# A batched mixture-of-experts kernel: the planner's part closed after two loads, semaphores by hand, experts in pairs, TensorE in one loop

## The chip, the cores and the metric

The kernel runs on one core of a Trainium2 chip. A core has five engines with instruction streams of their own: TensorE (PE; its weight loads are listed as PEld), VectorE (DVE), ScalarE (ACT), GpSimd (POOL) and SyncE (SP). Data comes from and goes to the chip's main memory (HBM) through 16 DMA engines. [...] The metric is the device time of one execution in microseconds (us), lower is better.

## The reference

There are 8 experts. Each multiplies its 256 rows of 512 numbers by its own first matrix, clips at zero, and multiplies by its own second matrix. Everything arrives and leaves as float32.

```python
n_experts, capacity, hidden, expert_hidden = 8, 256, 512, 2048
# x: (8, 256, 512)   w1: (8, 512, 2048)   w2: (8, 2048, 512), float32
h = np.matmul(x, w1)
h = np.maximum(h, 0)
return np.matmul(h, w2).astype(np.float32)
```

Per expert, `w1` and `w2` have 4.19 MB each. All weights together are 67.1 MB, `x` is 4.19 MB and the output is 4.19 MB.

## The kernel before

The kernel is written in Tile, a layer that allocates buffers from pools, finds the dependences between instructions and adds the semaphore waits. `manual_schedule` (line 48) keeps the instructions of each engine in the order of the source, so the order of the calls in lines 144 to 192 is the order of the queues.

A weight matrix is one load: 128 partitions, each with 32 KB of float32 that is contiguous in HBM, written to SBUF as bfloat16 (16 KB per partition, 2048 KB in all). `load_w1` (line 67) and `load_w2` (line 71) issue these loads on POOL. `wpool` gives each of the two tags three buffers (`WB = 3`), so a load waits until the expert three before it has been used. Only the last two `w2` are cut in two (line 73): expert 6 after 8 of its 16 blocks, expert 7 after 9.

`x` is taken in four groups (line 34). Experts 0 and 1 come as float32 on SP into `x_f` and are cast to bfloat16 by ACT (lines 145, 155, 156). Experts 2 and 3, and then 4 to 7, come on POOL with the cast made by the DMA (line 65). `transpose_x` (line 77) turns the blocks of `x` with TensorE, 64 transposes in all, and DVE or ACT copy them from PSUM to `xt`.

`first_layer(e)` (line 102) makes the hidden values in four steps of 16 matmuls; after each step ACT or DVE applies the clipping while it moves the result from PSUM to `ht`. `second_layer(e)` (line 124) runs 32 matmuls over the 16 blocks of `w2`, then DVE and ACT copy the two halves of the output to `o_sb`. For most experts the second layer follows the first. At the end all first layers are done before: 5, 6, 7 first layers, then second layers 5, 6, 7 (lines 183 to 191), and the loads stand in the same order: `w1` of 5, 6 and 7, then `w2` of 5, 6 and 7.

The output leaves in three stores: experts 0 to 4 and 5 to 6 on POOL, where they stand behind all loads of weights (lines 187 and 190), and expert 7 on SP (line 192). When the function returns, Tile closes: SP waits for every semaphore in use, then all engines meet at two barriers with the semaphores cleared in between (line 218).

TensorE's stream is unrolled: 832 matmuls (64 transposes, 512 of the first layer, 256 of the second), each with a weight load of its own, 1664 instructions.

Of the kernel before, what the change touches and what calls it, by code (L numbers as in the profile page):

```python
# [7 lines left out]


@with_exitstack  # L10
def kernel(
    ctx: ExitStack,
    tc: tile.TileContext,
    x: bass.AP,
    w1: bass.AP,
    w2: bass.AP,
    out: bass.AP,
):
    nc = tc.nc
    P = 128  # L20
    bf = mybir.dt.bfloat16
    f32 = mybir.dt.float32
    relu = mybir.ActivationFunctionType.Relu

    E, C, H = x.shape
    F = w1.shape[2]
    MT = C // P
    KT1 = H // P
    KT2 = F // P
    FB = 4  # L30
    WB = 3


    GROUPS = ((0, 1), (1, 1), (2, 2), (4, 4))


    w1_r = w1.rearrange("e (p kt) n -> e p kt n", p=P)
    w2_r = w2.rearrange("e (p kt) n -> e p kt n", p=P)
    out_r = out.rearrange("e (p mt) n -> p e mt n", p=P)

    const = ctx.enter_context(tc.tile_pool(name="const", bufs=1))
    wpool = ctx.enter_context(tc.tile_pool(name="weights", bufs=WB))
    hpool = ctx.enter_context(tc.tile_pool(name="hidden", bufs=3))
    ps_h = ctx.enter_context(tc.tile_pool(name="ps_h", bufs=2, space=bass.MemoryType.PSUM))
    ps_o = ctx.enter_context(tc.tile_pool(name="ps_o", bufs=4, space=bass.MemoryType.PSUM))


    ctx.enter_context(tc.manual_schedule())

    w1_sb, w2_sb, ht = {}, {}, {}  # L50
    group_of = {e: g for g, (e0, n) in enumerate(GROUPS) for e in range(e0, e0 + n)}
    x_f = const.tile([P, 2, MT, H], f32, name="x_f")
    x_b = [const.tile([P, n * MT, H], bf, name=f"x_b{g}") for g, (_, n) in enumerate(GROUPS)]
    xt = [const.tile([P, KT1, MT, n * P], bf, name=f"xt{g}") for g, (_, n) in enumerate(GROUPS)]
    o_sb = const.tile([P, E, MT, H], f32, name="out_sb")
    identity = const.tile([P, P], bf, name="identity")

    def x_rows(g):
        e0, n = GROUPS[g]
        return x[e0:e0 + n].rearrange("e c k -> (e c) k").rearrange(  # L60
            "(p j) k -> p j k", p=P
        )

    def load_x(g):
        nc.gpsimd.dma_start(x_b[g][:], x_rows(g))  # L65

    def load_w1(e):
        w1_sb[e] = wpool.tile([P, KT1, F], bf, tag="w1", name="w1_sb")
        nc.gpsimd.dma_start(w1_sb[e][:], w1_r[e])  # L69

    def load_w2(e):
        w2_sb[e] = wpool.tile([P, KT2, H], bf, tag="w2", name="w2_sb")
        cuts = {E - 2: (0, 8, 16), E - 1: (0, 9, 16)}.get(e, (0, KT2))
        for lo, hi in zip(cuts, cuts[1:]):
            nc.gpsimd.dma_start(w2_sb[e][:, lo:hi, :], w2_r[e, :, lo:hi, :])  # L75

    def transpose_x(g, blocks=None):


        n = GROUPS[g][1]  # L80
        J = n * MT
        KB = 8 // J
        for b in blocks if blocks is not None else range(KT1 // KB):
            pt = ps_o.tile([P, KB, J, P], bf, tag="ps_o", name="pt_tr")
            for i in range(KB):
                for j in range(J):
                    nc.tensor.transpose(  # L87
                        pt[:, i, j, :], x_b[g][:, j, b * KB + i::KT1], identity[:]
                    )
            for i in range(KB) if n > 1 else (slice(0, KB),):  # L90
                if n > 1:
                    src = pt[:, i].rearrange("p (l m) q -> p l m q", m=MT)
                    dst = xt[g][:, b * KB + i].rearrange("p m (q l) -> p l m q", l=n)
                    flip = b * KB + i
                else:
                    src, dst, flip = pt[:, i], xt[g][:], g
                if flip % 2:
                    nc.scalar.copy(dst, src)  # L98
                else:
                    nc.vector.tensor_copy(dst, src)  # L100

    def first_layer(e, between=()):
        g = group_of[e]
        i0 = (e - GROUPS[g][0]) * P
        ht[e] = hpool.tile([P, KT2, C], bf, tag="ht", name="ht_sb")
        for q in range(KT2 // FB):
            ph = ps_h.tile([P, FB, C], f32, tag="ps_h", name="pt_h")
            for i in range(FB):
                for kt in range(KT1):
                    nc.tensor.matmul(  # L110
                        ph[:, i, :],
                        w1_sb[e][:, kt, FB * q + i::KT2],
                        xt[g][:, kt, :, i0:i0 + P],
                        start=(kt == 0),
                        stop=(kt == KT1 - 1),
                    )
            if q % 2:
                nc.vector.tensor_relu(ht[e][:, FB * q:FB * (q + 1), :], ph[:])  # L118
            else:
                nc.scalar.activation(ht[e][:, FB * q:FB * (q + 1), :], ph[:], relu)  # L120
            if between:
                between.pop(0)()

    def second_layer(e):
        po = [
            ps_o.tile([P, H], f32, tag="ps_o", name=f"pt_o{mt}") for mt in range(MT)
        ]
        for kt in range(KT2):
            for mt in range(MT):
                nc.tensor.matmul(  # L130
                    po[mt][:],
                    ht[e][:, kt, mt * P:(mt + 1) * P],
                    w2_sb[e][:, kt, :],
                    start=(kt == 0),
                    stop=(kt == KT2 - 1),
                )
        nc.vector.tensor_copy(o_sb[:, e, 0, :], po[0][:])  # L137
        nc.scalar.copy(o_sb[:, e, 1, :], po[1][:])  # L138

    def store(e0, e1):  # L140
        nc.gpsimd.dma_start(out_r[:, e0:e1], o_sb[:, e0:e1])  # L141


    for e in (0, 1):
        nc.sync.dma_start(x_f[:, e], x_rows(e))
    load_w1(0)
    make_identity(nc, identity)
    load_w2(0)
    load_x(2)
    load_w1(1)  # L150
    load_w2(1)
    load_x(3)
    load_w1(2)
    load_w2(2)
    nc.scalar.copy(x_b[0][:], x_f[:, 0])  # L155
    nc.scalar.copy(x_b[1][:], x_f[:, 1])  # L156
    transpose_x(0)

    first_layer(0)
    load_w1(3)  # L160
    transpose_x(1)
    second_layer(0)
    load_w2(3)
    first_layer(1)
    load_w1(4)
    transpose_x(2)
    second_layer(1)
    load_w2(4)
    first_layer(2, [lambda kt=kt: transpose_x(3, [kt]) for kt in range(KT1)])
    load_w1(5)  # L170
    second_layer(2)
    first_layer(3)
    load_w1(6)
    second_layer(3)
    first_layer(4)
    load_w1(7)
    load_w2(5)
    load_w2(6)
    second_layer(4)
    load_w2(7)  # L180


    for e in (5, 6, 7):
        first_layer(e)


    store(0, 5)
    second_layer(5)
    second_layer(6)
    store(5, 7)  # L190
    second_layer(7)
    nc.sync.dma_start(out_r[:, 7], o_sb[:, 7])


# [28 lines left out]
```

## Time and profile before

| | us |
|---|---|
| median of 3 runs (lowest, highest) | 182.62 (182.59, 183.62) |
| span of the profiled execution, first to last instruction | 180.5 |
| TensorE busy with matmuls | 127.1 |
| ScalarE busy | 31.6 |
| VectorE busy | 31.8 |
| GpSimd busy | 13.1 |

The times are whole executions. The span runs from the first to the last instruction of the program, and the difference, 2.1 us against the median, lies around the span. In the views below a releaser is what ended a wait, "xN" is a number of instructions, and a DMA share of 1.00 means that all 16 DMA engines have work all the time. GB/s counts bytes as they are written, so a load that turns float32 into bfloat16 reads twice what the column shows.

### The profile page before, as it was taken

Reading aid. Unit: us, or ns where it says so; the run is one execution under the profiler, and the core shown is the slowest. Engines: PE = TensorE matmul, PEld = TensorE weight load, DVE = VectorE, ACT = ScalarE, POOL = GpSimd, SP = SyncE. Lnnn points to the kernel's source line nnn. Section 1 sums busy time; section 2 is a strip of 40 time slices with the busy share of each in tenths; the row PEclk is TensorE's granted clock in tenths of the full one; section 3 lists DMA queues with packets and bytes.
Section 4 is the critical chain, followed back from the end, with each engine's and each line's share of the span. In section 5 each row is a group of like instructions: output and inputs, shape, how many; then the busy total and the mean of one; then the engine's idle time right before and its main releaser. Section 6 shows DMA issues by size and latency. Waiting matters only on the chain.

```text
span 180.5 us, 1824 instructions
## 1 busy us (share of the span) xinstructions
PE 127.1 (70%) x832; PEld 89.1 (49%) x832; DVE 31.8 (18%) x29; ACT 31.6 (18%) x32; POOL 13.1 (7%) x28
## 2 busy tenths in 40 slices
PE   0206989059992199978778594979498968997910
PEld 0105964049840189538633591449387953442400
DVE  0100220102401028510501022012204230101010
ACT  3300230102221027512201130012122220101010
POOL 7300010100101000100100004030000000001000
PEclk9999999957999669999999997899969999999995
DMA  6998999999999899999999998999999999999994
GB/s 222 243 229 178 232 232 200 207 232 207 200 232 229 182 229 232 214 192 232 229 200 211 232 225 185 229 232 214 192 232 229 192 218 207 225 211 206 369 421 184
DMA packets 4246, 40.47 MB, mean 224 GB/s; under 512 B 400, under 2 KB 400, under 8 KB 1936
## 3 DMA queue, kind: packets, MB, share of 16 engines
q0 software_dynamic: 3808, 38.80, 96.9%
q1 hardware_dynamic: 432, 1.57, 2.3%
q8 instruction: 6, 0.10, 0.2%
HBM read 71.30 MB, written 4.19 MB: 418 GB/s over the span
## 4 chain that ended last, share of the span: by engine, by line
DMA 46%; PE 38%; another core or an unknown queue 9%; POOL 2%; issue 1%; ACT 0%; POOLq 0%
DMA w_sb<-in_w_dram 46%; PE pt_o L130 18%; PE pt_h L110 18%; PE pt_tr L87 2%; POOL w_sb L75 1%; POOL w_sb L69 0%; ACT out_sb L138 0%; POOL x_b L65 0%; POOL identity masks.py:199 0%; POOL identity masks.py:197 0%; POOLq masks.py:199 0%; POOLq L207 0%
## 5 line engine op out<-in xcount | busy, mean ns | idle before, releaser
L110 PE MATMUL pt_h<-xt,w_sb 128*128 128x256 bf16 x512 | 65.3, 293 | 30.7 <-DMA w_sb<-in_w_dram 30.7
L110 PEld LDWEIGHTS <-w_sb 128*128 128x128 bf16 x512 | 59.7, 147 | 36.9 <-DMA w_sb<-in_w_dram 33.9
L130 PE MATMUL pt_o<-w_sb,ht_sb 128*128 128x512 bf16 x256 | 58.2, 387 | 9.4 <-DMA w_sb<-in_w_dram 9.4
L130 PEld LDWEIGHTS <-ht_sb 128*128 128x128 bf16 x256 | 25.2, 99 | 40.6 <-issue 11.3
L118 DVE TENSOR_SCALAR ht_sb<-pt_h 128x1024 bf16<-128x1024 f32 x16 | 19.6, 1228 | 65.8 <-PE pt_h L110 65.8
L120 ACT ACTIVATE ht_sb<-pt_h 128x1024 bf16<-128x1024 f32 x16 | 16.5, 1032 | 69.2 <-PE pt_h L110 69.2
L138 ACT COPY out_sb<-pt_o 128x512 f32<-128x512 f32 x8 | 4.7, 585 | 62.5 <-PE pt_o L130 62.5
L137 DVE COPY out_sb<-pt_o 128x512 f32<-128x512 f32 x8 | 5.5, 692 | 57.2 <-PE pt_o L130 57.2
L69 POOL DMA_DIRECT2D w_sb<-in_w_dram x8 | 4.5, 556 | 85.3 <-PE pt_h L110 84.5
L100 DVE COPY xt<-pt_tr 128x1024 bf16<-128x1024 bf16 (+1 forms) x5 | 7.1, 1446 | 18.0 <-PE pt_tr L87 18.0
L87 PE MATMUL pt_tr<-identity,x_b 128*128 128x128 bf16 x64 | 5.4, 238 | 5.1 <-ACT x_b L155 5.1
L98 ACT COPY xt<-pt_tr 128x1024 bf16<-128x1024 bf16 (+1 forms) x5 | 7.4, 1502 | 6.6 <-PE pt_tr L87 4.0
L87 PEld LDWEIGHTS <-x_b 128*128 128x128 bf16 x64 | 4.9, 120 | 5.2 <-ACT x_b L155 5.1
L75 POOL DMA_DIRECT2D w_sb<-in_w_dram x10 | 5.4, 549 | 23.8 <-PE pt_o L130 23.8
L141 POOL DMA_DIRECT2D out_dram<-out_sb x2 | 1.6, 820 | 42.9 <-ACT out_sb L138 42.7
L155 ACT ACT_TABLE_LOAD x1 | 1.3, 1283 | 0.7 <-PEq L207 0.7
L155 ACT CAST x_b<-x_f 128x1024 bf16<-128x1024 f32 x1 | 1.0, 1044 | 2.0 <-DMA x_f<-in_x_dram 2.0
L65 POOL DMA_DIRECT2D x_b<-in_x_dram x2 | 1.1, 552 | 0.0
L156 ACT CAST x_b<-x_f 128x1024 bf16<-128x1024 f32 x1 | 1.0, 1044 | 0.2 <-DMA x_f<-in_x_dram 0.2
masks.py:199 POOL TENSOR_SCALAR_AFFINE_SELECT identity<-identity 128x128 bf16<-128x128 bf16 x1 | 0.3, 287 | 0.1
masks.py:197 POOL MEMSET identity<- 128x128 bf16 x1 | 0.2, 223 | 0.0
L207 POOL MEMSET const-float32-0.0<- 128x1 f32 x1 | 0.1, 93 | 0.2 <-issue 0.2
(3 smaller groups left out, 0.3 us busy)
## 6 DMA issues: line engine op xcount, KB each, us to landing
w_sb<-in_w_dram POOLq DMA_DIRECT2D x14, 2048.0 KB, 45.5
out_dram<-out_sb POOLq DMA_DIRECT2D x1, 2560.0 KB, 54.2
w_sb<-in_w_dram POOLq DMA_DIRECT2D x2, 1024.0 KB, 46.9
w_sb<-in_w_dram POOLq DMA_DIRECT2D x1, 1152.0 KB, 44.9
x_f<-in_x_dram SPq DMA_DIRECT2D x2, 512.0 KB, 3.7
x_b<-in_x_dram POOLq DMA_DIRECT2D x1, 1024.0 KB, 48.0
out_dram<-out_sb POOLq DMA_DIRECT2D x1, 1024.0 KB, 14.1
w_sb<-in_w_dram POOLq DMA_DIRECT2D x1, 896.0 KB, 48.8
```

The lines of the kernel that those rows point to most:

```text
L69: nc.gpsimd.dma_start(w1_sb[e][:], w1_r[e])
L75: nc.gpsimd.dma_start(w2_sb[e][:, lo:hi, :], w2_r[e, :, lo:hi, :])
L87: nc.tensor.transpose(pt[:, i, j, :], x_b[g][:, j, b * KB + i::KT1], identity[:])
L98: nc.scalar.copy(dst, src)
L100: nc.vector.tensor_copy(dst, src)
L110: nc.tensor.matmul(ph[:, i, :], w1_sb[e][:, kt, FB * q + i::KT2], xt[g][:, kt, :, i0:i0 + P], start=(kt == 0), stop=(kt == KT1 - 1),)
L118: nc.vector.tensor_relu(ht[e][:, FB * q:FB * (q + 1), :], ph[:])
L120: nc.scalar.activation(ht[e][:, FB * q:FB * (q + 1), :], ph[:], relu)
L130: nc.tensor.matmul(po[mt][:], ht[e][:, kt, mt * P:(mt + 1) * P], w2_sb[e][:, kt, :], start=(kt == 0), stop=(kt == KT2 - 1),)
L137: nc.vector.tensor_copy(o_sb[:, e, 0, :], po[0][:])
L138: nc.scalar.copy(o_sb[:, e, 1, :], po[1][:])
L155: nc.scalar.copy(x_b[0][:], x_f[:, 0])
```

## The change

Only two loads are left to Tile, the first two of `x`, and Tile is closed right behind them. Its closing block (here one drain more on SP and two barriers of all engines) thus stands near the start of the program. Everything else is issued behind it with semaphores that the kernel names itself, buffers at fixed addresses, and nothing at the end but SP's waits for the three stores.

- **x.** Four loads of 1 MB, float32, all on SP; one load covers two experts. The first two are issued ahead of the closing block, the other two behind it. ACT and DVE cast half of each to bfloat16, one pair ahead.
- **Experts two by two.** For each of four pairs: transposes of both experts' `x`, first layer of both, second layer of both. POOL issues the loads in the order `w1`, `w1`, `w2`, `w2`, with two buffers for each, so a load waits for the same matrix of the pair before. Only `w2` of expert 7 is cut (after 9 blocks).
- **TensorE.** One loop of four passes whose body holds 16 transposes, 128 matmuls of the first layer and 64 of the second, with the same addresses in each pass. As the counts can't differ between passes, each wait takes its number back off the semaphore (`take`). SP waits for each landed weight and passes it on as one count in `t_w`.
- **Stores.** Experts 0 to 3 and 4 to 6 on POOL, behind all loads; expert 7 on SP.

```diff
-    ctx.enter_context(tc.manual_schedule())
+    w_sb = [sbuf(f"w_sb{i}", (F * KT1,), bf) for i in range(4)]
+    ht = [sbuf(f"ht{i}", (KT2, C), bf) for i in range(2)]
...
-    def load_x(g):
-        nc.gpsimd.dma_start(x_b[g][:], x_rows(g))
+    def load_x(g):
+        return nc.sync.dma_start(x_f[:, g, :], x_r[g]).then_inc(s_x[g], 16)
+
+    for g in (0, 1):
+        tc.no_tile_sem_insts.add(load_x(g).ins.name)
+    tc.close()
+    tc.compile()
+    for g in range(2, NP):
+        load_x(g)
...
+    for p in range(NP):
+        for i in range(4):
+            e, b = 2 * p + i % 2, i % 2
+            if p:
+                pool.wait_ge(s_pe, at_h(p - 1, b, NQ - 1) if i < 2 else at_o(p - 1, b))
+            src = (w1_r if i < 2 else w2_r)[e]
+            if e == E - 1 and i == 3:
+                c = CUT * H
+                pool.dma_start(w_sb[i][:, :c], src[:, :c]).then_inc(s_w[i], 16)
+                pool.dma_start(w_sb[i][:, c:], src[:, c:]).then_inc(s_cut, 16)
+            else:
+                pool.dma_start(w_sb[i][:], src).then_inc(s_w[i], 16)
...
+    pool.wait_ge(s_pe, at_o(NP - 2, 1))
+    pool.dma_start(out_r[:, 0:4], o_sb[:, 0:4]).then_inc(s_out[0], 16)
+    pool.wait_ge(s_fin[0], 2)
+    pool.dma_start(out_r[:, 4:7], o_sb[:, 4:7]).then_inc(s_out[1], 16)
...
+    for p in range(NP):
+        for i in range(4):
+            sp.wait_ge(s_w[i], 16 * (p + 1))
+            cut = p == NP - 1 and i == 3
+            sp.sem_inc(t_w, 2 if i == 3 and not cut else 1)
...
+    sp.wait_ge(s_fin[1], 2)
+    sp.dma_start(out_r[:, E - 1], o_sb[:, E - 1]).then_inc(s_out[2], 16)
+    for s in s_out:
+        sp.wait_ge(s, 16)
...
+    def take(s, n):
+        pe.sem_inc(s, -n).wait_op(s, n, "sem-ge")
...
+    with pe.Fori(0, NP):
+        take(t_x, 2)
+        for h in range(2):
+            take(t_h[h], 1)
...
+                mm = pe.transpose(dst[:, n * P:(n + 1) * P], x_b[:, j, k::KT1], identity[:])
+            mm.then_inc(s_pe, 1)
+        for b in range(2):
+            take(t_w, 1)
+            for q in range(NQ):
+                take(t_h[q % 2], 1)
...
+        for b in range(2):
+            take(t_w, 1)
+            take(t_o[b], 2)
...
+            for kt in range(KT2):
+                if b and kt == CUT:
+                    take(t_w, 1)
```

The matmuls themselves are the same in number, shape and type.

More of the change, by code (lines that the diff above doesn't have):

```diff
@@ L5 @@
 from concourse import mybir
-from concourse.masks import make_identity
 from concourse._compat import with_exitstack
@@ L30 @@
     FB = 4
[L31 to L38, printed above, removed]
-    out_r = out.rearrange("e (p mt) n -> p e mt n", p=P)
[L41 to L44, printed above, removed]
@@ L45 @@
-    ps_o = ctx.enter_context(tc.tile_pool(name="ps_o", bufs=4, space=bass.MemoryType.PSUM))
-    ctx.enter_context(tc.manual_schedule())
[L50 to L62, printed above, removed]
-    def load_x(g):
-        nc.gpsimd.dma_start(x_b[g][:], x_rows(g))
[L67 to L88, printed above, removed]
-                    )
[L90 to L191, printed above, removed]
@@ new lines @@
+    x_f = sbuf("x_f", (NP, J * H), f32)
+    x_b = sbuf("x_b", (J, H), bf)
+    xt = sbuf("xt", (KT1, MT, 2 * P), bf)
+    w_sb = [sbuf(f"w_sb{i}", (F * KT1,), bf) for i in range(4)]
+    ht = [sbuf(f"ht{i}", (KT2, C), bf) for i in range(2)]
+    o_sb = sbuf("out_sb", (E, MT, H), f32)
+    identity = sbuf("identity", (P,), bf)
+    ph = [nc.alloc_psum_tensor(f"pt_h{i}", (P, FB, C), f32) for i in range(2)]
+    po = [nc.alloc_psum_tensor(f"pt_o{i}", (P, H), f32) for i in range(4)]
+    w1_sb = [w_sb[i][:].rearrange("p (kt n) -> p kt n", n=F) for i in range(2)]
@@ new lines @@
+    w2_sb = [w_sb[2 + i][:].rearrange("p (kt n) -> p kt n", n=H) for i in range(2)]
+    ptr = nc.alloc_psum_tensor
+    s_x = [sem(f"s_x{g}") for g in range(NP)]
+    s_w = [sem(f"s_w{i}") for i in range(4)]
+    s_cut = sem("s_cut")
+    s_id = sem("s_id")
+    s_out = [sem(f"s_out{i}") for i in range(3)]
+    s_pe = sem("s_pe")
+    t_x = sem("t_x")
+    t_w = sem("t_w")
+    t_h = [sem("t_h0"), sem("t_h1")]
+    t_o = [sem("t_o0"), sem("t_o1")]
+    s_fin = [sem("s_fin0"), sem("s_fin1")]
+    def load_x(g):
+        return nc.sync.dma_start(x_f[:, g, :], x_r[g]).then_inc(s_x[g], 16)
@@ new lines @@
+    for g in (0, 1):
[4 more added lines that the diff above has]
+        load_x(g)
+    STEPS = 2 + 2 * NQ + 2
+    at_t = lambda p, i: STEPS * p + 1 + i
+    at_h = lambda p, b, q: STEPS * p + 3 + NQ * b + q
+    at_o = lambda p, b: STEPS * p + 3 + 2 * NQ + b
+    pool = nc.gpsimd
+    for p in range(NP):
[10 more added lines that the diff above has]
+                pool.dma_start(w_sb[i][:], src).then_inc(s_w[i], 16)
+            if p == 0 and i == 0:
+                pool.memset(identity[:], 0.0).then_inc(s_id, 1)
+                pool.wait_ge(s_id, 1)
+                pool.affine_select(
+                    out=identity[:], in_=identity[:],
+                    compare_op=mybir.AluOpType.not_equal, fill=1.0, base=0,
+                    pattern=[[-1, P]], channel_multiplier=1,
+                ).then_inc(s_id, 1)
@@ new lines, with cast @@
+    sp.wait_ge(s_fin[1], 2)
+    sp.dma_start(out_r[:, E - 1], o_sb[:, E - 1]).then_inc(s_out[2], 16)
+    for s in s_out:
+        sp.wait_ge(s, 16)
+    for who, (eng, copy, act) in enumerate((
+        (nc.scalar, nc.scalar.copy, lambda o, i: nc.scalar.activation(o, i, relu)),
+        (nc.vector, nc.vector.tensor_copy, nc.vector.tensor_relu),
+    )):
+        half = slice(who * J // 2, (who + 1) * J // 2)
+        def cast(g):
+            eng.wait_ge(s_x[g], 16)
+            if g:
+                eng.wait_ge(s_pe, at_t(g - 1, 1))
+            src = x_f[:, g, :].rearrange("p (j k) -> p j k", j=J)
+            copy(x_b[:, half, :], src[:, half, :]).then_inc(t_x, 1)
+        cast(0)
+        for p in range(NP):
+            eng.wait_ge(s_pe, at_t(p, who))
+            src = ph[who][:].bitcast(bf).rearrange("p a b -> p (a b)")[:, :KT1 // 2 * J * P]
+            for k in range(KT1 // 2):
+                part = src[:, k * J * P:(k + 1) * J * P].rearrange(
+                    "p (l m q) -> p l m q", l=2, m=MT
+                )
+                dst = xt[:, who * KT1 // 2 + k].rearrange("p m (q l) -> p l m q", l=2)
+                last = copy(dst, part)
+            last.then_inc(t_h[who], 1)
+            if p + 1 < NP:
+                cast(p + 1)
+            for b in range(2):
+                for q in range(who, NQ, 2):
+                    eng.wait_ge(s_pe, at_h(p, b, q))
+                    act(ht[b][:, FB * q:FB * (q + 1), :], ph[q % 2][:]).then_inc(t_h[who], 1)
+            for b in range(2):
+                eng.wait_ge(s_pe, at_o(p, b))
+                done = s_fin[b] if p == NP - 1 else t_o[b]
+                copy(o_sb[:, 2 * p + b, who, :], po[2 * b + who][:]).then_inc(done, 1)
@@ new lines @@
+    pe = nc.tensor
+    def take(s, n):
+        pe.sem_inc(s, -n).wait_op(s, n, "sem-ge")
+    for s in t_h:
+        pe.sem_inc(s, 1)
+    for s in t_o:
+        pe.sem_inc(s, 2)
+    pe.wait_ge(s_id, 2)
+    with pe.Fori(0, NP):
+        take(t_x, 2)
+        for h in range(2):
+            take(t_h[h], 1)
+            dst = ph[h][:].bitcast(bf).rearrange("p a b -> p (a b)")
+            for n in range(KT1 // 2 * J):
+                k, j = h * KT1 // 2 + n // J, n % J
+                mm = pe.transpose(dst[:, n * P:(n + 1) * P], x_b[:, j, k::KT1], identity[:])
+            mm.then_inc(s_pe, 1)
+        for b in range(2):
+            take(t_w, 1)
+            for q in range(NQ):
+                take(t_h[q % 2], 1)
+                if b == 0 and q == 0:
+                    pe.wait_ge(t_h[1], 1)
+                for i in range(FB):
+                    for kt in range(KT1):
+                        mm = pe.matmul(
+                            ph[q % 2][:, i, :],
+                            w1_sb[b][:, kt, FB * q + i::KT2],
+                            xt[:, kt, :, b * P:(b + 1) * P],
+                            start=(kt == 0),
+                            stop=(kt == KT1 - 1),
+                        )
+                mm.then_inc(s_pe, 1)
+        for b in range(2):
+            take(t_w, 1)
+            take(t_o[b], 2)
+            if b:
+                for s in t_h:
+                    pe.wait_ge(s, 1)
+            for kt in range(KT2):
+                if b and kt == CUT:
+                    take(t_w, 1)
+                for mt in range(MT):
+                    mm = pe.matmul(
+                        po[2 * b + mt][:],
+                        ht[b][:, kt, mt * P:(mt + 1) * P],
+                        w2_sb[b][:, kt, :],
+                        start=(kt == 0),
+                        stop=(kt == KT2 - 1),
+                    )
+            mm.then_inc(s_pe, 1)
```

16 lines of the change are left out of this document (15 added, 1 removed).

## The prediction

> **What bounds the kernel now.** I read the busy shares first, then the DMA queues.
>
> ```profile
> span 180.5 us, 1824 instructions
> PE 127.1 (70%) x832; PEld 89.1 (49%) x832; DVE 31.8 (18%) x29; ACT 31.6 (18%) x32; POOL 13.1 (7%) x28
> q0 software_dynamic: 3808, 38.80, 96.9%
> q1 hardware_dynamic: 432, 1.57, 2.3%
> q8 instruction: 6, 0.10, 0.2%
> ```
>
> No engine is full, but the three DMA queues add up to 99.4% of 16 engines' span: this kernel is its transfers. The chain of waits says the same from the other side:
>
> ```profile
> 81.77 7.21 PE pt_h L110 x64
> 88.98 2.45 another core or an unknown queue
> 91.48 7.07 PE pt_o L130 x32
> 98.54 2.55 another core or an unknown queue
> 101.14 7.21 PE pt_h L110 x64
> 108.35 2.43 another core or an unknown queue
> 110.82 8.72 PE pt_o L130 x32
> ...
> 120.35 48.76 DMA w_sb<-in_w_dram
> 169.11 0.04 issue
> 169.15 3.20 PE pt_o L130 x14
> ```
>
> TensorE starts a layer every 9.7 us (81.77, 91.48, 101.14, 110.82), when a weight has landed, needs 7.2 or 7.07 us for it and waits some 2.5. The last part of the last weight lands at 169.11. What ends there shows in the DMA share of stretches of time (last three columns: granted clock, DMA share, GB/s written):
>
> ```profile
> 0.50:1.75 1.25, 0.00 (x0) 0.00 (x0) 0.00 (x0) 1.01 (x1) 0.49 (x1) 1.00 0.00 0
> 3.00:4.00 1.00, 0.00 (x0) 0.00 (x0) 0.00 (x0) 0.00 (x0) 1.00 (x3) 1.00 1.04 418
> 100.00:140.00 40.00, 32.09 (x225) 25.45 (x226) 7.67 (x7) 6.72 (x7) 4.07 (x7) 0.91 1.01 216
> 177.00:177.50 0.50, 0.00 (x0) 0.00 (x0) 0.00 (x0) 0.00 (x0) 0.00 (x0) 0.50 1.01 418
> 177.50:178.00 0.50, 0.00 (x0) 0.00 (x0) 0.00 (x0) 0.00 (x0) 0.00 (x0) 0.50 0.43 172
> 178.00:178.50 0.50, 0.00 (x0) 0.00 (x0) 0.00 (x0) 0.00 (x0) 0.00 (x0) 0.50 0.40 164
> 178.50:179.00 0.50, 0.00 (x0) 0.00 (x0) 0.00 (x0) 0.00 (x0) 0.00 (x0) 0.50 0.07 25
> 179.00:180.50 1.50, 0.00 (x0) 0.00 (x0) 0.00 (x0) 0.00 (x0) 0.00 (x0) 0.50 0.00 0
> ```
>
> The engines are full until 177.5. Then the share falls to 0.4, as if 6 of the 16 had about 1 us more to do, and from 179 nothing moves. So the time has four terms: the start until the first byte (1.75), the bytes, a ragged end (1 us), a closing piece without transfers (1.4). Overlap in the middle is worth nothing while the queues stay full.
>
> **The closing piece.** Issues of SP and POOL by time, time from issue to landing, and the waits of SP's own queue:
>
> ```profile
> 0.74 0.85 SPq L145 DMA_DIRECT2D x_f<-in_x_dram  x2
> 1.26 0.68 POOL L69 DMA_DIRECT2D w_sb<-in_w_dram  x1 [0.81 <-POOLq L207]
> 172.98 0.35 SPq L192 DMA_DIRECT2D out_dram<-out_sb  x1
> ...
> x_f<-in_x_dram SPq DMA_DIRECT2D x2, 512.0 KB, 3.7
> out_dram<-out_sb SPq DMA_DIRECT2D x1, 512.0 KB, 6.1
> ...
> SPq L218 <- PEq L218: 1.1, 2, 0.7
> L218 SPq EVENT_SEMAPHORE  x9: 17/28/28, 175.4 to 180.4; - x9
> L218 POOLq DRAIN  x3: 45/102/15062, 164.6 to 180.2; - x3
> ```
>
> The last store lands at 172.98 + 6.1 = 179.1; the span ends at 180.5. Those 1.4 us are Tile's close, 1.1 of them its two barriers. The change puts them at the start and leaves SP's waits, for which I allow 0.1: **-1.3**. One doubt: a POOL drain that began at 164.6 lasted 15.06 us, to 179.7, past the last landing by 0.6. If whatever follows the program drains POOL too, 0.6 of the gain moves out of the span into the 2.1 us around it; if engines that finish early can do their part of it sooner, some more is gained. The 1.3 is measured and nothing of the rest is, so I take 0 and keep -0.3 to +0.6.
>
> **The close at the start.** SP issues two loads of 1 MB at 0.74 as now (0.85 for both), then come 1.1 us of barriers before POOL's first weight, so that is issued near 0.74 + 0.85 + 1.1 = 2.7 instead of 1.26. Today's first layer begins at 15.2:
>
> ```profile
> L110 PE MATMUL pt_h<-xt,w_sb x512: 272/273/439, 15.2 to 146.8; 128*128 128x256 bf16 x171
> ```
>
> Its weight started to move at about 15.2 - 9.7 = 5.5, at most 4.2 us after its issue. In the changed kernel that is 2.7 + 4.2 = 6.9. The 2.1 MB ahead of it take 2.1 / 0.418 = 5.0 us from 1.75, until 6.8, and SP's other two loads, also issued near 2.7, need only some 1 us to start (0.74 to 1.75) and hold the engines for another 5. No gap: **0**. Without that cover, the delay of 1.4 us of POOL's issue would count in full.
>
> **x as float32.** The bytes read are the same 4.19 MB; what changes is their pace. Float32 to float32 ran at 418 GB/s written. Casting loads, with hardly anything else between 100 and 140, wrote 216 and so read 432. After: 4.19 / 0.418 = 10.0 us. Before: 1.05 / 0.418 + 1.57 / 0.216 = 2.5 + 7.3 = 9.8. Difference **+0.2**. The lower end is 0 (bytes read decide). The upper end comes from the second queue's row: 1.57 MB in 2.3% of 180.5, 4.15 us, is 379 GB/s, and 3.15 MB more at that pace are 8.3 against 7.3: +1.0. I take +0.2, from the stretch that shows just this kind of load alone. That x now comes ahead of the weights only delays the first layer.
>
> **Pairs, two buffers, POOL's waits.** A load now waits for the same matrix of the pair before. It has three other weights ahead of it: it is issued 7.2 us after its predecessor landed and needed 3 x 9.7 = 29.1 after that landing. The lead of 21.9 covers the 4.2 to start a load and 17 us of a late TensorE. Behind each such wait stand POOL's later loads and, last, its two stores; they wait in that order anyway. SP's new waits (17 to 28 ns each) pass a landed weight on; behind them stands only its last store, which needs all of them. TensorE's own waits, some 20 a pass, cost 0.04 us where one ended (the 0.04 at 169.11), under 1 us a pass. TensorE's pair costs 16 transposes (0.238 x 16 = 3.8 at most, by the row below), 2 x 7.21 and 2 x 7.07, together 32.4, with its waits 33.4, of the 38.8 us that four weights take. ACT and DVE get eight half casts of about 1 us on engines 18% busy. **0**.
>
> ```profile
> L87 PE MATMUL pt_tr<-identity,x_b 128*128 128x128 bf16 x64 | 5.4, 238 | 5.1 <-ACT x_b L155 5.1
> L98 ACT COPY xt<-pt_tr 128x1024 bf16<-128x1024 bf16 x3 | 6.0, 2014 | 4.0 <-PE pt_tr L87 4.0
> ```
>
> At a pass's turn the transposes stand behind the last second layer, and the first layer waits for them (some 1 us) and for copies as large as that 2.0: 3 us where 9.7 - 7.07 = 2.6 are free. That is 0.4 late, made good at the next weight.
>
> **The tail.** `w2` of expert 6 isn't halved any more, so its second layer no longer starts at half.
>
> ```profile
> 164.80 4.06 PE L130 MATMUL pt_o<-w_sb,ht_sb 128*128 128x512 bf16 x18 [1.23 <-DMA w_sb<-in_w_dram]
> ```
>
> Expert 7's first part, 9/16 of a weight (5.5 us), landed by 164.80, so expert 6's whole `w2` had landed by 159.3. From there 2 x 7.07 = 14.1 us: TensorE ends at 173.5 instead of 172.35, and the store is issued at 174.1 instead of 172.98. An issue needs 3.7 us with the queue empty (x_f), so it would land at 177.8, and before 179.1 the engines have the other stores anyway. Off the path, up to an issue at 179.1 - 3.7 = 175.4.
>
> The clock can push it over. After the wait of 2.43 us at 108.35 the second layer took 8.72, with this clock:
>
> ```profile
> 110.76:114.17 3.41, 3.35 (x8) 1.16 (x8) 0.00 (x0) 0.00 (x0) 0.01 (x1) 0.50 0.97 207
> ```
>
> After 2.45 and 2.55 it took 7.07 and 7.21. If that happens before expert 6, the issue comes at 174.1 + 1.65 = 175.8, 0.4 past the bound. One in three: **+0.1**. [...]
>
> **Instruction fetch.** 1664 matmuls and weight loads came with 6 instruction packets, 0.10 MB, so about 277 instructions per 16 KB packet. 0.2% of 16 x 180.5 us, over 6, is 0.96 us of one DMA engine for each. Six packets of nearly 1 us and six engines that end 1 us late: I read the ragged end as these packets. The loop's body has 416 such instructions and some 20 waits, more than one packet, so at least one packet still comes while the engines are full, and one suffices to make the last engine late. **0** if no engine gets two.
>
> **Sum.** 180.5 - 1.3 + 0.2 + 0.1 = 179.5, and 2.1 around it: **181.6**, 0.6% under the median of 182.62.
>
> **Rivals.**
> - *The loop fetches again in each pass, on the same DMA engines.* Its 436 instructions are 1.6 packets; three turns may bring the first one back three times, at 0.96 each. It decides from the second packet on one engine: 181.6 + 0.96 = 182.6 is no change, three more give 181.6 + 2.9 = **184.5**, slower. For it: six packets in one straight run, so code is fetched as it is reached. Against: no engine had two, and nothing in the trace shows a backward branch. [...]
> - *No packet while the engines are full.* All end together: 181.6 - 1.0 = **180.6**. Against: the body is longer than one packet.
> - *SP's drain waits for its loads.* Then barriers begin near 7.2 and SP's next load moves at 7.2 + 1.1 + 1.0 = 9.3 instead of following at 6.8: **184.1**. For it: POOL's 15 us drain, which followed that engine's stores. Against: nothing; no drain of SP with loads under way is in the trace.
> - *TensorE late at the end.* With the clock lost for both last layers the issue comes at 174.1 + 2 x 1.65 = 177.4, lands alone at 181.1, 2.0 past 179.1: 181.6 - 0.1 + 2.0 = **183.5**. Against: of three layers after such waits one lost its clock.
> - *x at 379 GB/s*: +0.8, **182.4**.
>
> **How the numbers follow.** Forecast 0.55, with its own range 181.0 to 182.2: below, x at 0, the tail at 0 and the 0.3 of the closing piece; above, its 0.6. First rival 0.12, spread evenly from 182.6 to 184.5; second 0.10; third 0.06; fourth 0.06; fifth 0.08; 0.03 for what I don't see. From 180.6 to 183.6 leaves out the upper half of the first (0.06), the third (0.06), half of the second's spread (0.03) and the unseen: 0.18. A change within 1% (180.8 to 184.4) is about what a measurement of this kernel can't tell from none. Faster: the second rival, 0.08 from the forecast's lower edge, and the unseen, 0.20. Slower: the top of the first, half of the third and some of the fourth, 0.12. Same: 0.68.
>
> **What would show it.** Right: DMA full from 2 to about 177.5, nothing after SP's last wait, weights every 9.7 us. The instruction packets and the time for which the share stays at a few sixteenths at the end tell the next: 1 us for the forecast, up to 3 for the first rival, none for the second. A share under 1 between 6 and 10 us is the third. A last store that runs alone is the fourth. Wrong altogether if a weight's cadence isn't 9.7.

## The result and the profile after

| | before | after |
|---|---|---|
| median (lowest to highest), us | 182.67 (182.59 to 183.62), 4 runs | 180.70 (180.50 to 181.06), 4 runs |
| ratio, with its 95% interval | | 0.9897 (0.9862 to 0.9933) |
| span of the profiled execution, us | 180.5 | 179.4 |

The kernel is about 1% faster. The time lies in the range given (180.6 to 183.6), but 0.9 us under the forecast of 181.6 and under the forecast's own range (181.0 to 182.2). It is just below the 180.8 that the prediction set as the limit of "within 1%"; the interval reaches to both sides of that limit. The span of 179.4 is within 0.1 of the 179.5 that the sum gave, so most of the error must lie outside the span; the experiments say where.

First the page of the changed kernel: its head, the row of the DMA share, the three queues (packets, MB, share of 16 engines' span), and the issues (count, KB each, us from issue to landing).

```profile
span 179.4 us, 1911 instructions
...
DMA  5999999999999999999999999999999999999996
...
q0 software_dynamic: 3376, 37.23, 92.8%
q1 hardware_dynamic: 720, 4.72, 6.7%
q8 instruction: 1, 0.02, 0.0%
...
x_f<-in_x_dram SPq DMA_DIRECT2D x4, 1024.0 KB, 17.5
...
out_dram<-out_sb SPq DMA_DIRECT2D x1, 512.0 KB, 4.7
```

The queues still add up to 99.5% of the span: the kernel is its transfers, as before. One instruction packet is left of six. Then three views of the same kernel: SP's waits (us in total, times, longest), its last two waits (line 133: durations in ns, first and last start), and the barriers that now stand at the start (line 83).

```profile
SPq L133 <- DMA out_dram<-out_sb: 4.3, 2, 3.1
```

```profile
L133 SPq EVENT_SEMAPHORE  x2: 17/22/28, 178.2 to 179.4; - x2
```

```profile
L83 POOLq EVENT_SEMAPHORE  x4: 17/17/17, 1.9 to 2.3; - x4
L83 SPq DRAIN  x3: 7/7/128, 1.6 to 2.1; - x3
```

Nothing follows SP's wait at 179.4, the end of the span; before, SP's waits for the stores were over at 179.1 and the span ended at 180.5. At the start SP's drain took 0.128 us with two loads under way, and the barriers were over at 2.3. Last the DMA share in stretches of time, the middle and the end (the last three columns are granted clock, DMA share and GB/s):

```profile
100.00:140.00 40.00, 32.10 (x222) 22.34 (x222) 8.50 (x10) 7.70 (x10) 2.16 (x5) 0.96 1.02 217
```

```profile
177.00:177.50 0.50, 0.00 (x0) 0.00 (x0) 0.00 (x0) 0.00 (x0) 0.00 (x0) 1.00 1.09 451
177.50:178.00 0.50, 0.00 (x0) 0.00 (x0) 0.00 (x0) 0.00 (x0) 0.00 (x0) 1.00 0.41 164
178.00:178.50 0.50, 0.00 (x0) 0.00 (x0) 0.00 (x0) 0.00 (x0) 0.00 (x0) 1.00 0.06 25
178.50:179.00 0.50, 0.00 (x0) 0.00 (x0) 0.00 (x0) 0.00 (x0) 0.00 (x0) 0.53 0.06 25
179.00:179.50 0.50, 0.00 (x0) 0.00 (x0) 0.00 (x0) 0.00 (x0) 0.00 (x0) 0.50 0.00 0
```

The middle is what it was (217 GB/s written, 216 before). At the end the share falls to 0.06, one sixteenth, and stays there for 1 us: one DMA engine is late, where six were. (The view names no engine; a sixteenth of the share is read as one engine.) In the trace the last weight lands at 169.38 instead of 169.11.

### The profile page after: what moved, and what is told of

Read it like the earlier page. It is cut to its first block, busy times and chain, and to the rows that moved or that the text cites. A ratio compares the mean times of both kernels' runs of the same rounds, so it can differ in the third digit from the quotient of the medians.

```text
span 179.4 us, 1911 instructions
## 1 busy us (share of the span) xinstructions
PE 126.0 (70%) x824; PEld 88.7 (49%) x832; DVE 33.1 (18%) x36; ACT 31.2 (17%) x37; POOL 11.4 (6%) x25
## 5 line engine op out<-in xcount | busy, mean ns | idle before, releaser
L199 PEld LDWEIGHTS pt_h<-xt,w_sb 128*128 128x128 bf16 x512 | 58.8, 146 | 26.4 <-issue 19.0
L217 PE MATMUL pt_o<-w_sb,ht 128*128 128x512 bf16 x248 | 58.5, 394 | 18.4 <-PEq L175 18.1
L217 PEld LDWEIGHTS pt_o<-w_sb,ht 128*128 128x128 bf16 x256 | 25.3, 101 | 50.5 <-issue 23.7
L165 DVE TENSOR_SCALAR ht<-pt_h 128x1024 bf16<-128x1024 f32 x16 | 19.6, 1225 | 60.8 <-PE pt_h L199 60.8
L137 ACT ACTIVATE ht<-pt_h 128x1024 bf16<-128x1024 f32 x16 | 16.4, 1024 | 56.4 <-PE pt_h L199 56.4
L189 PE MATMUL pt_h<-identity,x_b 128*128 128x128 bf16 x64 | 5.0, 241 | 7.2 <-PEq L175 7.2
L189 PEld LDWEIGHTS pt_h<-identity,x_b 128*128 128x128 bf16 x64 | 4.7, 121 | 7.8 <-issue 7.2
L158 DVE COPY xt<-pt_h 128x512 bf16<-128x512 bf16 x8 | 5.3, 717 | 3.0 <-PE pt_h L189 3.0
L158 ACT COPY xt<-pt_h 128x512 bf16<-128x512 bf16 x8 | 5.3, 732 | 1.3 <-PE pt_h L189 1.3
L147 DVE CAST x_b<-x_f 128x1024 bf16<-128x1024 f32 x4 | 2.8, 711 | 8.6 <-DMA x_f<-in_x_dram 8.6
```

The lines of the kernel that those rows point to most:

```text
L137: (nc.scalar, nc.scalar.copy, lambda o, i: nc.scalar.activation(o, i, relu)),
L147: copy(x_b[:, half, :], src[:, half, :]).then_inc(t_x, 1)
L158: last = copy(dst, part)
L165: act(ht[b][:, FB * q:FB * (q + 1), :], ph[q % 2][:]).then_inc(t_h[who], 1)
L189: mm = pe.transpose(dst[:, n * P:(n + 1) * P], x_b[:, j, k::KT1], identity[:])
L199: mm = pe.matmul(ph[q % 2][:, i, :], w1_sb[b][:, kt, FB * q + i::KT2], xt[:, kt, :, b * P:(b + 1) * P], start=(kt == 0), stop=(kt == KT1 - 1),
```

## The experiments

They are told in groups by question. Each group's runs stood beside fresh runs of the kernel before on the same chip. The median of the kernel before differs by up to 0.4 us between the groups (182.25 to 182.67), so the ratio to it is given beside each time; differences under about 0.3 us are not read.

### Does the ragged end come from the instruction packets, and is the loop itself worth time?

```diff
-    with pe.Fori(0, NP):
+    for _ in range(NP):
```

> TensorE's loop written out four times, nothing else changed. My theory: the time hangs on the last DMA engine, and one instruction packet makes it as late as six do, so the packets come back (6 or so, on different engines, as before) and the time stays at the changed kernel's 180.7 us, within 0.3. Rival (the loop itself is what the change gains by): the written-out kernel loses 0.9 us or more, 181.6 to 182.6.

Measured: 180.64 us, ratio 0.9895 (0.9871 to 0.9920), no difference from the changed kernel's 0.9897. Seven instruction packets came:

```profile
q8 instruction: 7, 0.11, 0.2%
```

The loop is not where the time went.

In the kernel before, the six packets moved at 29.34, 53.62, 77.88, 105.72, 129.98 and 148.75 us, and from one to the next TensorE ran some 235 to 295 of its matmuls and weight loads, about 255 on average. In the changed kernel the one packet moved at 35.95, in the first pass, and took 0.93 us.

The second kernel shortens TensorE's code by leaving work out (160 matmuls and weight loads and some 20 waits are left in the loop's body, fewer than the 255 or so that went with one packet), so its output is not the reference's; the third does the same with the loop written out (the first edit added to this one; the flags that close each sum are moved to match):

```diff
-                    for kt in range(KT1):
+                    for kt in range(1):
...
+                if kt % 2:
+                    continue
```

> Leaves out three quarters of the first layer's matmuls and half of the second layer's; loads, stores and waits are the same. [...] My theory: no instruction packet comes, no engine ends late, and the end moves forward by the packet's 0.93 us: 179.7 us. Rival (the late engine has another cause, or the end is set by the last store's own way): 180.7, with one engine still 1 us late.

> The same work left out, but TensorE's loop written out four times, some 750 instructions. My theory: two or three instruction packets while the engines are full, each on an engine of its own, so one late end of 0.93 us: 180.7 us, 1 us more than with the loop. Rival (the gain of the short loop comes from the work that was left out): both the same.

Measured: 179.76 us (0.9845, 0.9822 to 0.9868) with the loop, 180.79 (0.9902, 0.9877 to 0.9926) without. The queues of the first, and then the stretches at its end:

```profile
q0 software_dynamic: 3376, 37.23, 93.5%
q1 hardware_dynamic: 720, 4.72, 6.7%
```

```profile
177.00:177.50 0.50, 0.00 (x0) 0.00 (x0) 0.00 (x0) 0.00 (x0) 0.00 (x0) 0.50 0.99 402
177.50:178.00 0.50, 0.00 (x0) 0.00 (x0) 0.00 (x0) 0.00 (x0) 0.00 (x0) 0.50 0.14 49
178.00:178.50 0.50, 0.00 (x0) 0.00 (x0) 0.00 (x0) 0.00 (x0) 0.00 (x0) 0.50 0.00 0
```

The same two views of the second:

```profile
q8 instruction: 2, 0.03, 0.1%
```

```profile
178.00:178.50 0.50, 0.00 (x0) 0.00 (x0) 0.00 (x0) 0.00 (x0) 0.00 (x0) 0.50 0.12 49
178.50:179.00 0.50, 0.00 (x0) 0.00 (x0) 0.00 (x0) 0.00 (x0) 0.00 (x0) 0.50 0.06 25
```

No packet: the share goes to nothing within half a microsecond. Two packets: two sixteenths (0.12) for half a microsecond, then one. The two do the same work at the same mean clock (0.78) and differ by 1.0 us. As the loop alone made no difference above, this shows the cause of the ragged end, and that its length hangs on the latest engine and not on how many are late.

### What lies around the span?

```diff
     for s in s_out:
         sp.wait_ge(s, 16)
+    sp.sem_inc(s_end, 1)
...
+    for eng in (nc.gpsimd, nc.scalar, nc.vector, nc.tensor):
+        eng.wait_ge(s_end, 1)
```

> All four other engines wait at their end for a semaphore that SP gives after its last wait for a store. My theory: in the changed kernel the engines that are done early do their part of what follows the program while the stores still move; held back, they do it after them, and the time around the span goes from 1.3 us back to 2.1: 181.5 us with the same span plus 0.1. Rival (what follows the program begins only when all engines are done): 180.8.

Measured: 181.18 us (0.9929, 0.9901 to 0.9957), 0.5 more. Spans are unchanged, 179.1 to 179.4. What changed is time less span, run by run:

```
time less span, us (median)
kernel before, 58 runs           1.78  (1.72 to 1.84)
changed kernel, 4 runs           1.35  (1.26 to 1.50)
changed kernel, loop unrolled    1.40
all engines held to the end      1.79
```

The theory holds in kind: engines that are done early shorten what follows (1.35 us, against 1.79 when they are held). Its size was 0.45, not 0.85, because the kernel before had 1.78 around its span and not 2.1. The 2.1 had come from setting the median of some runs against the span of another, shorter one (over 58 runs the spans of the kernel before reach from 180.0 to 181.8, with a median of 180.7).

The closing piece itself, put back:

```diff
+    for _ in range(2):
+        nc.all_engine_barrier()
```

> The changed kernel with two barriers of all engines added at its end, behind SP's waits for the stores, as Tile's close has them. My theory: the last landing stays, the barriers and the drains add about 1 us to the span, and what follows the program takes 1.75 us instead of 1.4 as all engines end together: 182.1 us. Rival (the barriers themselves are cheap, as at the start, where the two took 0.5 us): 181.5.

Measured: 181.92 us (0.9969, 0.9948 to 0.9990), 1.2 more than the changed kernel: about 0.6 in the span (median 180.0), 0.55 around it (1.91). The span went as the rival said, the rest as the theory said. The barriers at the end of this kernel:

```profile
L226 POOLq EVENT_SEMAPHORE  x4: 17/17/17, 179.3 to 179.7; - x4
L226 POOLq DRAIN  x2: 47/5501/10955, 167.8 to 179.5; - x2
```

and the first of these two rows for the kernel before (that of its drain stands in the prediction):

```profile
L218 POOLq EVENT_SEMAPHORE  x4: 17/17/17, 179.7 to 180.4; - x4
```

In both, POOL drains from its last store issue on. Here the drain of 10.96 us is over at 178.8, before SP arrives at 179.3, and the two barriers take 0.55. In the kernel before, the drain of 15.06 us ended at 179.7, after SP had arrived at 179.2; in its second trace a drain of 13.49 us ended at 179.6, with SP there at 179.2 too. So, read from these traces, about half a microsecond of the 1.3 us removed was SP waiting for POOL's drain, and the rest barriers, other waits and the clearing of semaphores. No run takes the drain away alone.

### Is the close at the start free?

```diff
-    for g in (0, 1):
-        tc.no_tile_sem_insts.add(load_x(g).ins.name)
     tc.close()
     tc.compile()
-    for g in range(2, NP):
+    for g in range(NP):
```

> All loads of x behind Tile's close, none ahead of it. My theory: the close is free only because the first loads are under way; without them the first byte comes later by the drain and the two barriers, 0.7 us, and so does the end: 181.4 us. Rival (something else at the start, POOL's first weight or the filling of the engines, sets the pace): 180.7.

Measured: 181.19 us (0.9926, 0.9900 to 0.9953), 0.5 more, the span's median 179.85. In the trace the first byte moves at 2.41 instead of 1.77, 0.64 later. Cover matters, at about the price of the first byte. The profiled execution was the slowest of the six (181.76): it has a second instruction packet, at 177.4 us, after TensorE's last matmul. The median does not rest on it.

The other way round, Tile taken away:

```diff
-    for g in (0, 1):
-        tc.no_tile_sem_insts.add(load_x(g).ins.name)
-    tc.close()
-    tc.compile()
-    for g in range(2, NP):
+    for g in range(NP):
```

> The changed kernel without Tile: no close at the start at all, so no drains and no two barriers; all four loads of x follow each other on SP, and POOL issues its first weight some 1.5 us sooner. My theory (the prediction's 0): the close lies behind loads that keep the engines full, so nothing is gained: 180.7 us, with the one instruction packet at 36 us and one engine late as before. Rival (the barriers delay SP's third load and POOL's first weight so much that the engines fill up more slowly): up to 0.6 us less, 180.1.

Measured: 180.72 us (0.9915, 0.9894 to 0.9937). Nothing gained: behind loads under way, the close costs nothing that can be measured.

### Can the one packet be brought in early?

```diff
-    with pe.Fori(0, NP):
+    with pe.Fori(0, NP + 1) as turn, pe.If(turn > 0):
+        pe.wait_ge(s_id, 2)
```

The rest is the kernel without Tile, but for the four first counts, which TensorE gave itself and which come from ScalarE and VectorE here. TensorE makes one empty pass through its loop at the very start: it jumps from the loop's head over the whole body to its end, some 436 instructions on, more than the 255 or so that went with one packet, and back.

> [...] My theory: this jump brings the only instruction packet in at 1 to 2 us, before or while the DMA engines fill up, nothing is fetched later, no engine ends late, and the time falls by most of the packet's 0.93 us against the kernel without Tile: 179.8 to 180.0 us. Rival A (what is fetched then is gone by the time the loop reaches it): a second packet at 36 us and no gain, 180.7. Rival B (the early packet meets loads that are queued on its engine already): no packet at 36 us, but one engine still late, 180.7.

Measured: 180.95 us (0.9927, 0.9911 to 0.9943). Rival B. In the trace the jump is made at 1.0 us; the only packet moved at 4.51, among the loads of `x`, and none came later. The end:

```profile
178.00:178.50 0.50, 0.00 (x0) 0.00 (x0) 0.00 (x0) 0.00 (x0) 0.00 (x0) 0.86 1.00 410
178.50:179.00 0.50, 0.00 (x0) 0.00 (x0) 0.00 (x0) 0.00 (x0) 0.00 (x0) 0.50 0.14 49
179.00:179.50 0.50, 0.00 (x0) 0.00 (x0) 0.00 (x0) 0.00 (x0) 0.00 (x0) 0.50 0.02 8
```

One engine is still last, and the engines as a whole are full until 178.5, where the changed kernel's share falls before 178; why, no run settles. The compare-and-branch that jumped took 0.36 us (the loop's three later turns 0.21 to 0.22 each), and TensorE had run the code at the loop's end and turned back by 2.0 us. So it did not wait for that packet, and what the packet brought is not shown.

### Where does the lost 0.3 us of `x` lie?

The 0.3 is one trace against one: the last weight landed at 169.38 and at 169.11. In the traces of four more kernels with the same loads of `x` it landed at 169.20 (loop written out), 169.11 (engines held to the end), 169.19 (barriers put back) and 169.21 (without Tile), and in the second trace of the kernel before at 169.09. What is looked for here is therefore between 0 and 0.3 us.

GB/s in stretches of the start, the changed kernel:

```profile
1.75:2.25 0.50, 0.00 (x0) 0.00 (x0) 0.00 (x0) 0.00 (x0) 0.00 (x0) 1.00 0.90 131
2.25:2.75 0.50, 0.00 (x0) 0.00 (x0) 0.00 (x0) 0.37 (x1) 0.00 (x0) 1.00 0.95 164
2.75:3.25 0.50, 0.00 (x0) 0.00 (x0) 0.00 (x0) 0.50 (x1) 0.34 (x1) 1.00 0.50 213
3.25:3.75 0.50, 0.00 (x0) 0.00 (x0) 0.00 (x0) 0.41 (x1) 0.50 (x2) 1.00 1.08 459
...
5.25:6.25 1.00, 0.00 (x0) 0.00 (x0) 0.38 (x1) 0.38 (x1) 0.91 (x2) 1.00 0.99 418
```

and the kernel before:

```profile
1.75:2.25 0.50, 0.00 (x0) 0.00 (x0) 0.00 (x0) 0.27 (x1) 0.42 (x3) 1.00 1.07 188
2.25:2.75 0.50, 0.00 (x0) 0.00 (x0) 0.00 (x0) 0.00 (x0) 0.50 (x2) 1.00 0.85 336
2.75:3.25 0.50, 0.00 (x0) 0.00 (x0) 0.00 (x0) 0.00 (x0) 0.50 (x2) 1.00 1.04 426
```

Over the first 1.5 us the changed kernel moves (188 + 336 + 426 - 131 - 164 - 213) x 0.5 = 221 KB less, 0.5 us at 418. This trace is the extreme one: it moved 254 KB, the four other kernels just named 328 to 385, 0.2 to 0.35 us less than the kernel before. Its first load is 1 MB in packets of 8 KB, before it was 512 KB in packets of 4 KB. Three kernels tried that.

```diff
-        return nc.sync.dma_start(x_f[:, g, :], x_r[g]).then_inc(s_x[g], 16)
+        h = J * H // 2
+        return [
+            nc.sync.dma_start(x_f[:, g, c:c + h], x_r[g][:, c:c + h]).then_inc(s_x[g], 16)
+            for c in (0, h)
+        ]
```

> Each of the four float32 loads of x cut into two, with 4 KB per partition instead of 8 KB, as the kernel before had them. My theory: the 0.3 us by which the bytes of the changed kernel end later were lost at the start, where the engines fill up more slowly with 8 KB packets (404 GB/s is reached 1.5 us after the first byte instead of 0.75); with 4 KB packets the last landing is 0.3 us earlier: 180.4 us. Rival (my prediction's: float32 loads run at 418 where casting loads read 432, whatever their packets): no gain, 180.7.

Measured: 181.71 us (0.9956, 0.9939 to 0.9973): 1.0 slower, against both. It was not a clean test: it doubled the issues, and it takes 4 KB out of every 8 KB, which the kernel before did not. Its trace shows where time went:

```profile
5.25:6.25 1.00, 0.00 (x0) 0.00 (x0) 0.35 (x1) 0.35 (x1) 0.82 (x3) 1.00 0.99 360
6.25:7.25 1.00, 0.01 (x1) 0.04 (x2) 0.42 (x1) 0.69 (x1) 1.00 (x2) 1.00 1.01 352
```

The loads of `x` ran at 360 and 352 GB/s with every engine busy, against 418, and the first packet of a weight started at 8.0 us instead of 6.9. (This execution was the slowest of the twelve, 182.37. It also has a granted clock of 0.64 between 161 and 165 us, the last store issued at 177.3, and a second instruction packet at 177.8; whether the others had these is not known.) The next two keep each expert's half MB without gaps.

```diff
-    x_r = x.rearrange("(g e) c k -> g (e c k)", e=2).rearrange("g (p f) -> g p f", p=P)
+    x_r = x.rearrange("(g e) (p m) k -> g p e (m k)", e=2, p=P)
...
-                dst = xt[:, who * KT1 // 2 + k].rearrange("p m (q l) -> p l m q", l=2)
+                dst = xt[:, who * KT1 // 2 + k].rearrange("p m (l q) -> p l m q", l=2)
```

> The changed kernel with each load of x as 256 packets of 4 KB, one expert after the other and each expert's half MB without gaps, as the kernel before had them; the number of loads and the times of their issues stay. (The run with halves of each row took 4 KB out of every 8 KB, and twice the issues.) My theory, weakened by that run: the slow filling at the start comes from the 8 KB packets, and the last landing is 0.3 to 0.5 us earlier: 180.3 us. Rival (the filling varies by itself, or hangs on the number of loads on the ring): 180.7. If 4 KB packets as such are worse, it is slower, 181 or more.

Measured: 180.64 us (0.9913, 0.9896 to 0.9930), no gain, and the engines still fill slowly:

```profile
1.75:2.25 0.50, 0.00 (x0) 0.00 (x0) 0.00 (x0) 0.00 (x0) 0.00 (x0) 1.00 1.67 131
2.25:2.75 0.50, 0.00 (x0) 0.00 (x0) 0.00 (x0) 0.28 (x1) 0.00 (x0) 1.00 0.18 74
2.75:3.25 0.50, 0.00 (x0) 0.00 (x0) 0.00 (x0) 0.50 (x1) 0.25 (x1) 1.00 1.01 418
...
5.25:6.25 1.00, 0.00 (x0) 0.00 (x0) 0.68 (x1) 0.68 (x1) 1.00 (x2) 1.00 1.01 418
```

Packet size alone is not it. The last run adds the small first loads:

```diff
-    for g in (0, 1):
-        tc.no_tile_sem_insts.add(load_x(g).ins.name)
+    for e in range(2):
+        h = slice(e * MT * H, (e + 1) * MT * H)
+        half = nc.sync.dma_start(x_f[:, 0, h], x_r[0, :, e]).then_inc(s_x[0], 16)
+        tc.no_tile_sem_insts.add(half.ins.name)
```

> The changed kernel with the start of the kernel before: ahead of the close only the first pair's x, as two loads of 512 KB with 128 packets of 4 KB each, one for each expert; the other three loads of 1 MB (256 packets of 4 KB) stand behind the close. My theory: the engines fill up as in the kernel before (110 GB/s in the first quarter us, over 400 after 0.75 us, instead of 1.5 us), which gives back the 0.3 us by which the last weight landed later: 180.4 us. Rival A (the filling does not hang on the size of the first load): 180.7. Rival B (1 MB ahead of the close is too little cover, and the engines run dry before the third load starts): 181.0 or more, with a DMA share under 1 between 3 and 5 us.

Measured: 181.27 us (0.9939, 0.9918 to 0.9961), 0.6 slower. Its start:

```profile
1.75:2.25 0.50, 0.00 (x0) 0.00 (x0) 0.00 (x0) 0.00 (x0) 0.00 (x0) 1.00 0.92 238
2.25:2.75 0.50, 0.00 (x0) 0.00 (x0) 0.00 (x0) 0.35 (x1) 0.00 (x0) 1.00 0.90 352
2.75:3.25 0.50, 0.00 (x0) 0.00 (x0) 0.00 (x0) 0.50 (x1) 0.33 (x1) 1.00 1.05 426
...
4.25:5.25 1.00, 0.00 (x0) 0.00 (x0) 0.00 (x0) 0.00 (x0) 0.82 (x3) 1.00 1.01 365
5.25:6.25 1.00, 0.00 (x0) 0.00 (x0) 0.58 (x1) 0.58 (x1) 1.00 (x2) 1.00 1.01 377
```

The engines do fill as in the kernel before: in 1.5 us (238 + 352 + 426) x 0.5 = 508 KB, with 475 KB in the kernel before, 254 in the changed one and 312 in the run just told. The size of the first loads is not all of it: the kernel with halves of rows had first loads of 512 KB too and moved 365 KB, inside the 254 to 385 of the kernels with first loads of 1 MB. And the share stays at 1 while the pace drops to 365 and 377, against 401 and 418 in the same stretches of the changed kernel, and the gain is given back with more. Rival B is out (the share shows no gap). Why the same 4 KB packets ran at 418 in the run before this one and at 365 here is open.

### The kernel before once more

> The kernel before once more, unchanged. Its spans reached from 180.2 to 181.6 us in eleven runs, with a median of 180.9, while the profile that the prediction rests on has 180.5. My theory: in the longer ones one DMA engine gets two instruction packets and ends 1.9 instead of 1 us late, so a run of 181 or more shows one engine with nearly 2 us behind the others. Rival: TensorE loses its clock before the last layers and the last store comes late; then the share at the end is even, only later.

Its span was 180.3, a short one, so it tells nothing of the long ones. The spans of the kernel before spread over 1.8 us in 58 runs, those of the changed kernel over 0.8 (179.0 to 179.8) in only four; whether the two differ in this, and why, stays open.

None of these kernels that computes the whole output is measurably faster than the changed one.

## Why the prediction was right, and where its size was off

- **Bound by transfers:** held. Queues at 99.5%, 217 GB/s in the middle, and weights landing 9.7 us apart (140.27, 149.96, 159.64).
- **Closing piece, -1.3 in the span:** held. Last landing to end of span went from 180.46 - 179.09 = 1.37 to 179.43 - 179.38 = 0.05, so -1.32. Putting barriers back returned 0.6 of it; of the rest, about 0.5 went with POOL's long drain, by the traces. The prediction took the 1.1 us that SP waited at the barriers for their price. Put back without that drain in the way, they kept SP waiting for 0.4.
- **Around the span, "I take 0 and keep -0.3":** this is the step whose size failed, and it accounts for some 0.75 of the 0.9 between forecast and result: 1.35 us lay around the span, not 2.1. About 0.45 was real: engines that end early shorten what follows, and holding them back returned it (1.35 to 1.79). The prediction had named it and left it out of the sum, since no row gave it a size. Another 0.3 was a mistake of method: "2.1 around it" set one execution's span against the median of others; taken run by run it is 1.78.
- **The span, 179.5:** the level was met (179.4 in the profile, a median of 179.35 over the four runs), in part by luck. The sum starts from 180.5, a short span of the kernel before: the median of its 58 runs is 180.7. Against that the span fell by 1.35, where the sum has 1.0.
- **Close at the start, 0:** held. Without Tile 180.72. POOL issued its first weight at 2.90 (2.7 said). The cover is real too, though at 0.5 us, not the 1.4 of POOL's delay: with the loads of `x` moved behind the close, what came late was the first byte, by 0.64, not POOL's weight.
- **`x` as float32, +0.2:** the size is inside what the traces show (last weight 0 to 0.29 later), and the mechanism is not shown. Once running, the loads kept the 418 the sum used; but 0.2 to 0.5 us showed in the filling of the first 1.5 us, which the sum did not have, and part of it was made up later. No run separates the two. Both attempts to undo it by smaller loads were slower.
- **Pairs, two buffers, POOL's waits, 0:** nothing in the traces speaks against it. The loop written out took the same time.
- **Tail, +0.1:** the store was issued at 174.7 (174.1 said), and the clock was full at the end (1.00 from 159.9 to 174.0 us), so the term was 0. The bound of 175.4 was too strict. In the kernel with the loop written out the clock was down, as the prediction feared (0.57 between 159 and 163 us), and the store was issued at 176.1; it landed 3.1 us later, and the time was the same.

```profile
out_dram<-out_sb SPq DMA_DIRECT2D x1, 512.0 KB, 3.1
```

- **Instruction fetch, 0:** held, and its reading is now shown: one packet (0.93 us at 35.95) leaves an engine 1 us late, none brings 1.0 us. The first rival fell: four passes over a body of some 436 instructions brought one packet in the trace, and no turn of the loop a second. By its time alone the second rival (180.6) is nearer to the 180.70 than the forecast; that is chance, as a packet did come and an engine was late. With a body of some 180 instructions, which left work out, no packet came, and the time was 179.76. Bodies between these two lengths were not run.
- **SP's drain:** the third rival fell, 0.128 us with two loads under way.

## What to carry to other kernels

When a kernel is bound by its DMA engines, look at the last microsecond in sixteenths of the DMA share. Here a single 16 KB instruction packet on one engine ended the kernel 1 us later, seven packets cost no more than one (180.64 and 180.70 us), and only none gained (179.76). Work that only closes a program (barriers, drains, clearing semaphores) belongs behind loads that are already under way, and engines that have finished should be let go: that gained time both inside the span (1.32 us) and after it (0.45). Compare a span only with the time of the same execution, and a landing in one trace only with several traces of the other kernel: the 0.27 us of `x` in one trace was 0 to 0.29 over seven.

## What the runs showed that was not expected

- **After the span.** The time that follows the last instruction hangs on when the other engines end: 1.35 us when they end early, 1.79 when all are held to the end, 1.91 with barriers there.
- **Pace at the start.** In the first 1.5 us after the first byte, first loads of 512 KB on SP's queue moved 475 and 508 KB, and 365 when each took half of every row; first loads of 1 MB moved 254 to 385. In the two changed kernels with the small first loads the pace then fell to 352 to 377 GB/s, with every engine busy. A busy share of 1 does not mean full pace: from 5.25 to 6.25 us a share of 1.01 went with 377 GB/s in one run and with 418 in another.
- **A second packet.** The loop brought one instruction packet in most traces, but two in the profiled executions of two kernels (all of `x` behind the close, and `x` in halves of rows), the second at 177.4 and 177.8 us, behind TensorE's last matmul. Both were the slowest executions of their kernel, by 0.57 and 0.66 us over the median; what was fetched is not shown.
- **An early packet is not a free packet.** After the jump at 1.0 us the only instruction packet moved at 4.5 us, among the loads, and one engine was still late at the end.
